# Attention mix weights spread by repeating DMAs, with the attention's branch last of four

## Chip, core and metric

The kernel runs on one core of one Trainium2 chip. The metric is the device time of one execution in microseconds. The kernel before took a median of 1982.03 us in 3 runs (1981.79 to 1984.21).

## What is computed

Two layers of a mixer over 1024 tokens and 1024 channels. In each layer a normalised input `h` is projected once; the slices feed four token mixers (Fourier, convolution, dilated attention, pooling) and a SiLU gate path for each mixer. All is float32. The part that the change touches is how three attention groups are joined:

```python
def dilated_mixture(qkv, cos, sin):
    ...
    for g, (window, dil) in enumerate(DILATED_CFG):      # three groups
        o, l = dilated_window_attention(q[:, :, g], k[:, :, g], v[:, :, g], dil, window // (2 * dil))
        outs.append(o); lses.append(l)
    alpha = jax.nn.softmax(jnp.stack(lses, axis=0), axis=0)
    out = outs[0] * alpha[0][..., None]
    for g in range(1, N_ATT_GROUPS):
        out = out + outs[g] * alpha[g][..., None]

def hybrid_layer(...):
    ...
    for n, y in enumerate(branch_outs):                  # Fourier, convolution, attention, pooling
        y_n = (y * gate_paths[:, :, n]) @ w_branch[n]
        mg = jax.nn.sigmoid(h @ w_gate[n] + b_gate[n])
        merged = mg * y_n if merged is None else merged + mg * y_n
    return x + merged @ w_out
```

`alpha` is one number per group, token and head, and each is multiplied with 64 channels of that head.

## The kernel before

Activations lie with channels on the 128 partitions and tokens along the free dimension, in two halves of 512 tokens. Every matmul in full precision is three float32r passes over a high and a low part; `split` (L104) makes these parts with one ScalarE copy and one VectorE subtraction, and is what `w`, `g`, `t`, `pl` and `wf` on L106 and L107 are.

The order within a layer (`layer`, L1161) is: the pooling and convolution inputs, six attention groups (two head pairs `hp` times three dilations `g`; each has a `q`, a `k` and a `v` unit), two Fourier units, six gate paths, four branch projections (`branch`, L951), the merge gates (`gates`, L1029) and the output projection. These main matmuls are emitted in a plain loop. All that does not lie on this main line is a generator in a lane: `pool`, `taps` (the convolution's 31 taps on VectorE, then `conv_mix` for each half), `att` (`att_tiles`: scores, softmax and weighted values of one group), `mix` (`att_mix`), `fou`, `g` (the gated input of a branch) and `forms` (sums and differences of `h` for the gates). `passes` (L124) calls `tick` after every second pair of operands, which are 6 matmuls, and a tick advances each lane by one `yield`. `finish` steps a lane to its end on the spot. The planner that puts the emitted instructions into the queues of the engines takes the order of emission as priority; loads under `high_priority` go ahead of it.

One head pair's statistics are `st` [128 tokens, 8 tiles, maximum and sum for two heads]. The dilated groups have their tokens in another order, so `st` goes through a DRAM tile `sc` and back as `nat` in token order (L564 to L574). `att_mix` (L577) then works out the three weights `e` with tokens on the partitions. To multiply them with the outputs, whose partitions are channels, it copies each weight 64 times along the free dimension (`fx`, L609), and TensorE transposes these copies in blocks of 128 by 128, four for a half and group (`fb`, L615). VectorE multiplies the group's output `og`, read back from DRAM (`od`), with that PSUM tile (L616) and adds the groups up (L618). The result is parked in DRAM (`att`).

For the branches, `gated` (L927) loads a parked mixer output (`unpark`), multiplies it with its gate path where that has not been done (`gt`, for the attention alone) and splits it (`g`). `YORDER` sets the order of the branches, here pooling (3), Fourier (0), attention (2), convolution (1). Before branch `i` the lanes that make the input of the next one are finished and its `gated` is started, so it is emitted beside branch `i`. With the third branch (`FORMS = 2`) `token_forms` (L963) starts. `branch` evacuates each PSUM tile with ScalarE to `y` (L959) and stores it from SP (L960). PSUM has 3 banks `mm` and 5 `aux`; the SBUF tiles of 512 tokens are 12 slots of one tag, `t`.

Of the kernel before, what the change touches and what calls it, by code (L numbers as in the profile page):

```python
# [9 lines left out]
F32 = mybir.dt.float32  # L10
F32R = mybir.dt.float32r
AF = mybir.ActivationFunctionType
ALU = mybir.AluOpType

P = 128
S = 1024
# [12 lines left out]
TAP = 3  # L29
LEAD = 6  # L30
ORDER = (0, 2, 1, 3)
YORDER = (3, 0, 2, 1)
FORMS = 2
NW = 4
KEPT = (None, None, None, "H", "H", "H", "H", "M")
# [12 lines left out]
class Net:  # L48
# [404 lines left out]
                self.split(hi[:, cs], lo[:, cs], ps[:, :len(part) * P])  # L453
                yield

    def att_group(self, l, hp, g, done):
        cos, sin = self.slot("cos", tag="M"), self.slot("sin", tag="M")
        for i, t in enumerate((cos, sin)):
            self.nc.sync.dma_start(out=t, in_=self.a["rope"][g, i])
        q = self.rope_unit(l, U_Q + 2 * g + hp, g, cos, sin, True)  # L460
        k = self.rope_unit(l, U_K + 2 * g + hp, g, cos, sin, False)
        vt = self.v_unit(l, U_V + 2 * g + hp, g)
        self.start("att", self.att_tiles(l, hp, g, q, k, vt, done))

    def att_tiles(self, l, hp, g, q, k, vt, done):
        nc = self.nc
        v = {}
        yield from self.wait(2)
# [78 lines left out]
        ps, pts = {}, {}  # L547
        for t in range(8 + LAG):
            if t < 8 and t % 2 == 0:
                s = products(t)  # L550
                for i in range(2):
                    ps[t + i] = scores(t + i, s[i])
            yield
            if t >= LAG:
                weighted(t - LAG, *pts.pop(t - LAG))
            if LAGT <= t < 8 + LAGT:
                pts[t - LAGT] = transposed(t - LAGT, ps.pop(t - LAGT))
            yield
        od = self.dr.tile([P, S], F32, name=f"od_{l}_{hp}_{g}")
        nc.sync.dma_start(out=od, in_=o)  # L560
        if g == 0:
            done.append((od, st))
            return
        sc = self.dr.tile([S, 4], F32, name=f"sc_{l}_{hp}_{g}")  # L564
        if g == 1:
            dst = sc.rearrange("(j p r) c -> p r j c", p=P, r=4)
            for r in range(4):
# [4 lines left out]
                nc.sync.dma_start(out=dst[two], in_=st[64 * two:64 * two + 64])  # L572
        nat = self.sm.tile([P, 8, 4], F32, tag="nat", name=f"nat{g}", bufs=4)
        nc.sync.dma_start(out=nat, in_=sc.rearrange("(t p) c -> p t c", p=P))  # L574
        done.append((od, nat))

    def att_mix(self, groups, park):  # L577

        nc = self.nc
        while len(groups) < 3:  # L580
            yield
        yield from self.wait(4)
        sm = lambda nm: self.sm.tile([P, 8, 2], F32, tag="x" + nm, name="x" + nm, bufs=2)
        ms = [st[:, :, 0:2] for _, st in groups]
        ds = [st[:, :, 2:4] for _, st in groups]
        m = sm("m")
        nc.vector.tensor_tensor(out=m, in0=ms[0], in1=ms[1], op=ALU.max)
        nc.vector.tensor_tensor(out=m, in0=m, in1=ms[2], op=ALU.max)
        es = []
        for g in range(3):  # L590
            e = sm(f"e{g}")
            nc.vector.tensor_tensor(out=e, in0=ms[g], in1=m, op=ALU.subtract)
            nc.scalar.activation(out=e, in_=e, func=AF.Exp)
            es.append(e)
        z, t = sm("z"), sm("t")
        nc.vector.tensor_tensor(out=z, in0=ds[0], in1=es[0], op=ALU.mult)
        for g in (1, 2):
            nc.vector.tensor_tensor(out=t, in0=ds[g], in1=es[g], op=ALU.mult)
            nc.vector.tensor_tensor(out=z, in0=z, in1=t, op=ALU.add)
        nc.vector.reciprocal(out=z, in_=z)  # L600
        for g in range(3):
            nc.vector.tensor_tensor(out=es[g], in0=es[g], in1=z, op=ALU.mult)
        yield from self.wait(2)
        for hf in range(2):
            sl = slice(hf * H, hf * H + H)
            out = None
            for g in range(3):
                f = self.t2("fx").rearrange("p (t h c) -> p t h c", t=4, h=2)
                nc.vector.tensor_copy(out=f, in_=es[g][:, 4 * hf:4 * hf + 4].unsqueeze(3).to_broadcast([P, 4, 2, 64]))  # L609
                og = self.t2("og")  # L610
                nc.sync.dma_start(out=og, in_=groups[g][0][:, sl])
                yield from self.wait(4)
                ps = self.aux("fb")
                for j in range(4):
                    nc.tensor.transpose(ps[:, j * P:(j + 1) * P], f[:, j].rearrange("p h c -> p (h c)"), self.ident)  # L615
                nc.vector.tensor_tensor(out=og, in0=og, in1=ps, op=ALU.mult)  # L616
                if g:
                    nc.vector.tensor_tensor(out=out, in0=out, in1=og, op=ALU.add)  # L618
                else:
                    out = og  # L620
            nc.sync.dma_start(out=park[:, sl], in_=out)
# [539 lines left out]
    def layer(self, l):  # L1161
        nc = self.nc
        pool = self.pool(l)
        att = self.dr.tile([2, P, S], F32, name=f"att{l}")
        for hp in range(2):
            done = []
            for g in range(3):
                self.att_group(l, hp, g, done)
            self.start("mix", self.att_mix(done, att[hp]))
        uf = [self.fourier_in(l, c) for c in range(2)]  # L1170
        res, fy = [], []
        self.start("fou", self.fourier_pq(l, uf, res))
        self.start("fou", self.fourier_out(l, res, fy))
        conv = self.dr.tile([2, P, S], F32, name=f"conv{l}")
        gps = {0: [], 1: [], 2: []}
        four = self.dr.tile([2, P, S], F32, name=f"four{l}")
        self.start("fou", self.gate_later(fy, gps[0], four))
        for hf in range(2):
            self.start("taps", self.conv_mix(l, hf, gps[1], conv))
        tf = {i: [] for i in range(1, 5)}  # L1180
        g = {n: [] for n in range(4)}
        make = {0: self.gated(self.unpark(four), None, g[0]), 1: self.gated(self.unpark(conv), None, g[1]),
                2: self.gated(self.unpark(att), gps[2], g[2]), 3: self.gated(self.unpark(pool), None, g[3])}
        lanes = {0: ("fou",), 2: ("att", "mix"), 1: ("taps",), 3: ()}
        for n in GORDER:
            for c in range(2):
                if (n, c) == (GORDER[2], 1):
                    self.start("g", make[YORDER[0]])
                gps[n].append(self.gate_path(l, n, c))
        for i, n in enumerate(YORDER):  # L1190
            self.finish("g")
            if i < 3:
                for lane in lanes[YORDER[i + 1]]:
                    self.finish(lane)
                self.start("g", make[YORDER[i + 1]])
            if i == FORMS:
                self.start("forms", self.token_forms(tf))
            self.branch(l, n, g[n])
        self.finish("forms")
        self.out_proj(l, self.gates(l, tf))  # L1200
# [97 lines left out]
```

## Time and profile before

| | before |
|---|---|
| median of 3 runs | 1982.03 us |
| the profiled execution | 1983.95 us |
| its span, first to last instruction | 1982.2 us |
| TensorE busy | 1950.8 us (98%) |
| VectorE busy | 1485.8 us (75%) |
| ScalarE busy | 1001.1 us (51%) |
| mean granted TensorE clock | 0.998 of full speed |

The page of the profile gives the busy time of each engine, the costliest groups of instructions and the DMA issues. Matmuls overlap: what one costs TensorE is the distance to the start of the next, and not its busy time. A wait is the idle time of an engine just before an instruction, put down to what released it.

### The profile page before, as it was taken

What the parts mean: (1) busy time and instruction counts of PE and PEld (TensorE: products, weight loads), DVE (VectorE), ACT (ScalarE), POOL (GpSimd) and SP (SyncE); (2) the same over time, 40 slices, a digit from 0 to 9 for tenths busy, and PEclk for the clock granted to TensorE, in tenths of its full rate; (3) what the DMA queues carried; (4) which work ended last, traced back from release to release, by engine and by line L of the source; (5) the groups of instructions that cost most, each with busy time, mean ns of one, the idle gap of its engine ahead of it and who ended that gap; (6) DMA issues with size and microseconds to landing.
All of it is one profiled execution on the core that took longest, in us unless ns stands there. A gap on an engine that the chain in (4) does not pass through costs nothing.

```text
span 1982.2 us, 26843 instructions
## 1 busy us (share of the span) xinstructions
PE 1950.8 (98%) x9518; PEld 1629.6 (82%) x9518; DVE 1485.8 (75%) x2731; ACT 1001.1 (51%) x1911; POOL 41.2 (2%) x90
## 2 busy tenths in 40 slices
PE   9999999999999999999999999999999999999998
PEld 7788888788888888887888888888888888888788
DVE  8598888886587878776655888888564877787764
ACT  7335655567474434344421456656775644443441
POOL 0000000000000000000000000000000000000000
PEclk9999999999999999999999999999999999999999
DMA  7244343423874433427421534434248823434443
GB/s 239 78 150 125 104 131 110 129 73 102 265 277 164 143 107 113 155 79 259 161 79 50 156 119 133 131 106 114 75 148 293 282 88 125 138 98 147 169 150 107
DMA packets 129877, 281.07 MB, mean 142 GB/s; under 512 B 33360, under 2 KB 38352, under 8 KB 129744
## 3 DMA queue, kind: packets, MB, share of 16 engines
q1 hardware_dynamic: 116784, 237.29, 37.2%
q0 software_dynamic: 10944, 39.85, 6.0%
q10 hardware_dynamic: 2016, 2.23, 0.3%
q8 instruction: 75, 1.23, 0.3%
q14 instruction: 58, 0.48, 0.1%
HBM read 186.84 MB, written 67.30 MB: 128 GB/s over the span
## 4 chain that ended last, share of the span: by engine, by line
PE 82%; DVE 9%; ACT 4%; DMA 3%; issue 2%; SPq 0%; DVEq 0%; ACTq 0%
PE z L130 25%; PE ga L130 13%; PE g L130 9%; PE op L130 9%; PE gb L130 8%; PE py L130 8%; PE z L257 3%; DVE cv L870 2%; PE pv L130 2%; PE s L494 2%; PE pt L520 1%; DVE w L107 1%; ACT w L106 1%; DMA mt<-m 1%; ACT o L544 1%
## 5 line engine op out<-in xcount | busy, mean ns | idle before, releaser
L130 PE MATMUL z<-h,w 128*128 128x512 f32 x3000 | 739.6, 396 | 1.9 <-DVE gp L631 1.4
L130 PEld LDWEIGHTS z<-h,w 128*128 128x128 f32 x3000 | 547.9, 188 | 107.4 <-DVE gp L631 1.8
L107 DVE TENSOR_TENSOR w<-wr,w 128x1024 fp32r<-128x1024 f32 (+3 forms) x136 | 158.8, 1171 | 100.1 <-ACT w L106 90.9
L106 ACT ACTIVATE w<-wr 128x1024 fp32r<-128x1024 f32 (+3 forms) x136 | 137.9, 1016 | 170.4 <-PE z L130 79.3
L130 PE MATMUL gb<-t,wf 128*128 128x512 f32 x768 | 184.5, 389 | 0.0
L130 PE MATMUL g<-h,wf 128*128 128x512 f32 x768 | 184.5, 389 | 0.0
L130 PE MATMUL ga<-t,wf 128*128 128x512 f32 x768 | 184.5, 389 | 0.0
L130 PE MATMUL op<-m,w 128*128 128x512 f32 (+1 forms) x960 | 179.7, 348 | 2.4 <-DVE m L107 2.4
L870 DVE SCALAR_TENSOR_TENSOR cv<-cv,params 128x512 f32<-128x512 f32 x240 | 179.0, 746 | 2.2
L130 PE MATMUL py<-g,w 128*128 128x512 f32 x768 | 178.9, 392 | 1.1 <-DVE gp L631 0.5
L130 PEld LDWEIGHTS op<-m,w 128*128 128x128 f32 x960 | 154.0, 190 | 26.5 <-DVE m L107 3.7
L130 PEld LDWEIGHTS py<-g,w 128*128 128x128 f32 x768 | 143.2, 188 | 32.5 <-ACT y L959 2.2
L130 PEld LDWEIGHTS g<-h,wf 128*128 128x128 f32 x768 | 144.2, 188 | 29.9
L130 PEld LDWEIGHTS gb<-t,wf 128*128 128x128 f32 x768 | 144.2, 188 | 29.8
L130 PEld LDWEIGHTS ga<-t,wf 128*128 128x128 f32 x768 | 144.2, 188 | 29.8
L106 ACT ACTIVATE wf<-wr 128x512 fp32r<-128x512 f32 x144 | 90.9, 632 | 117.8 <-issue 46.5
L107 DVE TENSOR_TENSOR wf<-wr,wf 128x512 fp32r<-128x512 f32 x144 | 98.8, 686 | 19.6 <-ACT wf L106 18.4
L508 ACT ACTIVATE p<-p,nm 128x256 f32<-128x256 f32 (+1 forms) x192 | 88.8, 464 | 48.8 <-DVE nm L505 48.6
L106 ACT ACTIVATE wf<-s 128x512 fp32r<-128x512 f32 x64 | 40.4, 632 | 105.5 <-PE gb L130 62.9
L544 ACT ACTIVATE o<-pv 64x128 f32<-64x128 f32 x192 | 67.6, 352 | 50.3 <-PE pv L130 48.4
L130 PE MATMUL ga<-h,wf 128*128 128x512 f32 x384 | 92.3, 389 | 0.0
L130 PEld LDWEIGHTS ga<-h,wf 128*128 128x128 f32 x384 | 72.1, 188 | 14.9
(251 smaller groups left out, 2697.5 us busy)
## 6 DMA issues: line engine op xcount, KB each, us to landing
wr<-in_w_in_dram SPq DMA_DIRECT2D x74, 512.0 KB, 3.7
y<-y SPq DMA_DIRECT2D x128, 256.0 KB, 4.0
y<-y POOLq DMA_DIRECT2D x64, 512.0 KB, 4.8
wr<-in_w_gate_dram SPq DMA_DIRECT2D x48, 512.0 KB, 4.3
wr<-in_w_out_dram SPq DMA_DIRECT2D x32, 512.0 KB, 3.5
rot<-rt SPq DMA_DIRECT2D x192, 64.0 KB, 2.0
cv<-in_w_gate_dram SPq DMA_DIRECT2D x16, 512.0 KB, 5.1
wr<-in_w_branch_dram SPq DMA_DIRECT2D x16, 512.0 KB, 5.0
```

Source lines behind the costliest of these rows:

```text
L106: self.nc.scalar.activation(out=hi, in_=src, func=AF.Copy)
L107: self.nc.vector.tensor_tensor(out=lo, in0=src, in1=hi.bitcast(F32), op=ALU.subtract)
L130: self.nc.tensor.matmul(ps, w, x, start=(first and i + u == 0), stop=(i == n - 1 and u == 2), skip_group_check=open_)
L257: self.nc.tensor.matmul(ps, a[:, k], b, start=(k + j == 0), stop=(k == KC - 1 and j == 2))
L494: mm(s[i][h], q[h + j][:, qs], k[h][:, a:a + n], start=(j == 0), stop=(j == 2))
L508: nc.scalar.activation(out=ph, in_=ph, func=AF.Exp, bias=nm[:, h:h + 1], accum_out=st[:, t, 2 + h:3 + h])
L520: nc.tensor.transpose(pt[:, cs], p[:, off:off + P], self.ident)
L544: nc.scalar.activation(out=dst, in_=src, func=AF.Copy)
L870: self.tc.keep_in_program_order(nc.vector.scalar_tensor_tensor(out=y, in0=u[:, j:j + H], scalar=tap(j), in1=y, op0=ALU.mult, op1=ALU.add))
```

## The change

The softmax weights of a head pair (now one tile `ea` for three groups) are transposed once, [128 tokens, 48] to [48, 128 tokens], copied to SBUF (`er`) and stored in a DRAM tile `ed`, one row of 128 tokens for each group, tile and head. For each half and group two DMAs read the four rows of a head 64 times, so that `f` comes with channels on the partitions, and VectorE multiplies it with `og`. The `fx` copies and `fb` transposes are gone, and the three `Exp` are one. The token-order round trip of `st` becomes `by_token`, called after the last scores of a group (`t == 6`) instead of behind its last tile, so that `att_mix` waits for the statistics (`sts`) first and for the outputs (`done`) later. Its waits, in ticks, change. `YORDER` puts the convolution's branch third and the attention's last.

```diff
-YORDER = (3, 0, 2, 1)
+YORDER = (3, 0, 1, 2)
...
@@ att_tiles
                     ps[t + i] = scores(t + i, s[i])
+                if t == 6:
+                    self.by_token(st, f"{l}_{hp}_{g}", g, sts)
             yield
...
         nc.sync.dma_start(out=od, in_=o)
+        done.append(od)
+
+    def by_token(self, st, name, g, sts):
+        nc = self.nc
         if g == 0:
-            done.append((od, st))
+            sts.append(st)
             return
...
-        done.append((od, nat))
-
-    def att_mix(self, groups, park):
-        nc = self.nc
-        while len(groups) < 3:
+        sts.append(nat)
+
+    def att_mix(self, sts, groups, park, name):
+        nc = self.nc
+        while len(sts) < 3:
             yield
-        yield from self.wait(4)
+        yield from self.wait(10)
...
-        es = []
+        ea = self.sm.tile([P, 3, 8, 2], F32, tag="xe", name="xe", bufs=2)
+        es = [ea[:, g] for g in range(3)]
         for g in range(3):
-            e = sm(f"e{g}")
-            nc.vector.tensor_tensor(out=e, in0=ms[g], in1=m, op=ALU.subtract)
-            nc.scalar.activation(out=e, in_=e, func=AF.Exp)
-            es.append(e)
+            nc.vector.tensor_tensor(out=es[g], in0=ms[g], in1=m, op=ALU.subtract)
+        nc.scalar.activation(out=ea, in_=ea, func=AF.Exp)
...
-        yield from self.wait(2)
+        yield from self.wait(6)
+
+        ps = self.aux("et")
+        nc.tensor.transpose(ps[:48, 0:P], ea.rearrange("p g t h -> p (g t h)"), self.ident)
+        er = self.t2("er")
+        nc.scalar.activation(out=er[:48, 0:P], in_=ps[:48, 0:P], func=AF.Copy)
+        ed = self.dr.tile([3, 8, 2, P], F32, name=f"ed_{name}")
+        nc.sync.dma_start(out=ed.rearrange("g t h p -> (g t h) p"), in_=er[:48, 0:P])
+        while len(groups) < 3:
+            yield
         for hf in range(2):
             sl = slice(hf * H, hf * H + H)
             out = None
             for g in range(3):
-                f = self.t2("fx").rearrange("p (t h c) -> p t h c", t=4, h=2)
-                nc.vector.tensor_copy(out=f, in_=es[g][:, 4 * hf:4 * hf + 4].unsqueeze(3).to_broadcast([P, 4, 2, 64]))
-                og = self.t2("og")
-                nc.sync.dma_start(out=og, in_=groups[g][0][:, sl])
-                yield from self.wait(4)
-                ps = self.aux("fb")
-                for j in range(4):
-                    nc.tensor.transpose(ps[:, j * P:(j + 1) * P], f[:, j].rearrange("p h c -> p (h c)"), self.ident)
-                nc.vector.tensor_tensor(out=og, in0=og, in1=ps, op=ALU.mult)
+                f, og = self.t2("fx"), self.t2("og")
+                for h in range(2):
+                    nc.sync.dma_start(out=f[64 * h:64 * h + 64].rearrange("p (t n) -> p t n", n=P),
+                                      in_=ed[g, 4 * hf:4 * hf + 4, h].unsqueeze(0).to_broadcast([64, 4, P]))
+                nc.sync.dma_start(out=og, in_=groups[g][:, sl])
+                yield from self.wait(3 if hf or g else 6)
+                nc.vector.tensor_tensor(out=og, in0=og, in1=f, op=ALU.mult)
```

## Rows read from the trace of the kernel before

**Rows 1.** The page, busy time (share) and instructions of each engine.

```profile
PE 1950.8 (98%) x9518; PEld 1629.6 (82%) x9518; DVE 1485.8 (75%) x2731; ACT 1001.1 (51%) x1911; POOL 41.2 (2%) x90
```

**Rows 2.** Table by stretches: busy us (instructions) per engine, clock, DMA share, GB/s.

```profile
300.00:400.00 100.00, 97.45 (x534) 81.82 (x533) 83.15 (x195) 53.42 (x134) 0.00 (x0) 1.00 0.39 115
...
520.00:540.00 20.00, 20.00 (x96) 16.51 (x95) 7.69 (x11) 9.54 (x16) 0.00 (x0) 1.00 0.95 308
...
600.00:900.00 300.00, 300.00 (x1326) 248.54 (x1324) 232.56 (x357) 123.78 (x191) 17.48 (x33) 1.00 0.38 128
...
1540.00:1560.00 20.00, 20.00 (x90) 16.58 (x89) 20.00 (x34) 13.01 (x24) 1.06 (x2) 1.00 0.72 232
```

**Rows 3.** Waits of PE: who waited for whom, us in total, times, longest.

```profile
PE pv L130 <- DVE pl L107: 2.2, 3, 0.8
...
PE fb L615 <- DVE fx L609: 1.4, 2, 1.0
...
PE fb L615 <- ACT o L544: 0.8, 2, 0.4
...
PE py L130 <- ACT y L959: 0.4, 2, 0.2
```

**Rows 4.** Chain that ended last in order of time: start, us, what.

```profile
1523.78 48.58 PE py L130 x213
```

**Rows 5.** The tile `fb`: count, ns min/median/max, starts; then what waits ended on.

```profile
L615 PE MATMUL fb<-consts,fx x96: 269/273/332, 317.7 to 1506.2; 128*128 128x128 f32 x96
L616 DVE TENSOR_TENSOR og<-og,fb x24: 674/682/689, 319.5 to 1506.5; 128x512 f32<-128x512 f32 x24
...
  DMA og<-od: 5.9, 3
```

**Rows 6.** Timeline of PE, 1500 to 1530: start, us, instruction.

```profile
1505.90 0.60 PE L615 MATMUL fb<-consts,fx 128*128 128x128 f32 x4
1506.25 17.30 PE L130 MATMUL py<-g,w 128*128 128x512 f32 x75
```

**Rows 7.** The tile `xe`: its widening copy to `fx`.

```profile
L609 DVE COPY fx<-xe x24: 411/420/428, 313.3 to 1498.1; 128x512 f32<-128x512 f32 x24
```

**Rows 8.** DMA: queues, issues with median us to landing, then L611 (issue ns).

```profile
q1 hardware_dynamic: 116784, 237.29, 37.2%
...
q10 hardware_dynamic: 2016, 2.23, 0.3%
...
att<-og SPq DMA_DIRECT2D x8, 256.0 KB, 2.5
...
unpark<-att SPq DMA_DIRECT2D x8, 256.0 KB, 6.1
...
sc<-st SPq DMA_DIRECT2D x16, 4.0 KB, 1.6
...
L611 SPq DMA_DIRECT2D og<-od x24: 326/426/1108, 310.6 to 1501.2; - x24
...
DMA to landing us min/median/max: 2.6/3.8/6.9
```

**Rows 9.** Waits of SP's queue: us in total, times, longest.

```profile
SPq L117 <- DVE w L107: 301.8, 85, 23.6
...
SPq L568 <- DVE st L503: 42.5, 10, 13.0
```

**Rows 10.** Timeline of PE, 500 to 512: end of `conv_mix`, first branch.

```profile
503.31 0.40 PE L130 MATMUL cp<-csh,w 128*128 128x512 f32 x1
...
508.12 1.52 PE L130 MATMUL py<-g,w 128*128 128x512 f32 x6
```

**Rows 11.** DVE: the multiply `gt`, its wait (us, times, longest), first weight form.

```profile
L938 DVE TENSOR_TENSOR gt<-unpark,gp x8: 684/686/694, 538.8 to 1520.9; 128x512 f32<-128x512 f32 x8
...
DVE gt L938 <- DMA unpark<-att: 10.3, 3, 5.4
...
601.01 0.69 DVE L107 TENSOR_TENSOR wf<-s,wf 128x512 fp32r<-128x512 f32 x1 [5.05 <-ACT wf L106]
```

More of the change, by code (lines that the diff above doesn't have):

```diff
@@ L454, in v_tiles, with att_group @@
                 yield
-    def att_group(self, l, hp, g, done):
+    def att_group(self, l, hp, g, done, sts):
         cos, sin = self.slot("cos", tag="M"), self.slot("sin", tag="M")
@@ L462, in att_group, with att_tiles @@
         vt = self.v_unit(l, U_V + 2 * g + hp, g)
-        self.start("att", self.att_tiles(l, hp, g, q, k, vt, done))
-    def att_tiles(self, l, hp, g, q, k, vt, done):
+        self.start("att", self.att_tiles(l, hp, g, q, k, vt, done, sts))
+    def att_tiles(self, l, hp, g, q, k, vt, done, sts):
         nc = self.nc
@@ L560, in att_tiles @@
         nc.sync.dma_start(out=od, in_=o)
+        done.append(od)
+    def by_token(self, st, name, g, sts):
+        nc = self.nc
         if g == 0:
-            done.append((od, st))
+            sts.append(st)
             return
-        sc = self.dr.tile([S, 4], F32, name=f"sc_{l}_{hp}_{g}")
+        sc = self.dr.tile([S, 4], F32, name=f"sc_{name}")
         if g == 1:
@@ L574, in att_tiles @@
         nc.sync.dma_start(out=nat, in_=sc.rearrange("(t p) c -> p t c", p=P))
-        done.append((od, nat))
-    def att_mix(self, groups, park):
+        sts.append(nat)
+    def att_mix(self, sts, groups, park, name):
         nc = self.nc
-        while len(groups) < 3:
+        while len(sts) < 3:
             yield
-        yield from self.wait(4)
+        yield from self.wait(10)
         sm = lambda nm: self.sm.tile([P, 8, 2], F32, tag="x" + nm, name="x" + nm, bufs=2)
-        ms = [st[:, :, 0:2] for _, st in groups]
-        ds = [st[:, :, 2:4] for _, st in groups]
+        ms = [st[:, :, 0:2] for st in sts]
+        ds = [st[:, :, 2:4] for st in sts]
         m = sm("m")
@@ L1165, in layer @@
         for hp in range(2):
-            done = []
+            done, sts = [], []
             for g in range(3):
-                self.att_group(l, hp, g, done)
-            self.start("mix", self.att_mix(done, att[hp]))
+                self.att_group(l, hp, g, done, sts)
+            self.start("mix", self.att_mix(sts, done, att[hp], f"{l}_{hp}"))
         uf = [self.fourier_in(l, c) for c in range(2)]
```

## The prediction

> **What bounds the kernel now.** I read the page first: TensorE (PE) is busy for 1950.8 of 1982.2 us, VectorE (DVE) for 75% and ScalarE (ACT) for half [rows 1]. The table by stretches then shows where that holds [rows 2]: in the gates (600 to 900) PE is busy for all 300 us; in the attention (300 to 400) for 97.45 of 100 with DVE at 83; in the branch projections for 20.00 of 20 us both at 520 to 540, where the DMA engines are 0.95 busy, and at 1540 to 1560 in the second layer, where DVE too has 20.00 of 20. The granted clock is 1.00 in all of them, the 2.4 GHz level. PE's own waits are small: the largest that touch this change are 1.4 us for `fx`, 0.8 us for the evacuation that frees a bank for `fb`, and 0.4 us in `py` for `y` [rows 3]. So a PE instruction taken out is worth the time until the next one starts, and one more wait of PE costs its whole length.
>
> **How time is counted in the code.** All lanes advance by one yield per tick, and a tick comes once per 6 main matmuls. 213 `py` in 48.58 us [rows 4] give 0.228 us for one and 1.37 us for a tick. A half unit has 4 ticks, a branch 16. I count ticks from the start of the first attention unit in the first layer: six groups of 24 (144), two Fourier units (160), six gate paths (208), then four branches ending at 224, 240, 256 and 272.
>
> **Removed: the transposes.** 24 groups of four `fb` (96 in all) [rows 5]. One `fb` shows 273 ns busy, but they overlap. A group that starts at 1505.90 is followed by the next `py` at 1506.25 [rows 6]: four in 0.35 us, and the 24 pairs of this kind look alike. As the times are rounded I take 0.355: 24 x 0.355 = 8.5 us of PE. Where the page and the row differ: the Trainium skill ("TensorE: Matmul & The Clock Gate", Part 4: PE-mode transpose) puts a transpose in a kernel at some 275 ns; the busy time here agrees, the starts do not, at 89 ns each. By its figure the sum would start from an estimated 26 us.
>
> **Removed beside it.** 24 `fx` copies of 0.42 us leave DVE (10.1 us) [rows 7], and 8 of 12 small `Exp` leave ACT. DVE's multiply by `fb` stays, reading `f` from SBUF; `gt`, a multiply of two SBUF tiles of the same size, takes 0.686 us against its 0.682 [rows 5, 11], so no difference. The two waits of `fb`, 2.2 us in all [rows 3], go with it; what is late next there is `pv` or `pt`, whose inputs come from the same DVE and ACT. I count 1.0 us of it as gained, with bounds of 0 and 2.2. The lighter DVE might relieve PE's `pv` waits for `pl` (2.2 us [rows 3]); I count nothing, and up to 1.5 us in the range.
>
> **Added on PE and ACT.** Four transposes of 48 rows. No such operation is in the trace; the nearest is one `fb` (89 ns from start to start), and a lone one with nothing behind it could cost its 273 ns [rows 5]. Between 0 and 1.1 us; I take 4 x 0.09 = 0.4 us, since matmuls follow it directly. The four `er` copies on ACT stand against the eight `Exp`; 0.
>
> **Added on the queues.** Per mix 12 DMAs for `f` and one for `ed`, on SP: 52 in all. Issuing one `og` took a median of 0.43 us [rows 8], so 22 us of SP over the run, some 6 us per mix in about 29 us (21 ticks). Each `f` DMA writes 64 x 4 packets of 512 B: 12288 packets. Bounds: the SP queue's mean packet of 2.03 KB cost 0.372 x 16 x 1982.2 / 116784 = 101 ns; a quarter of it is 25 ns; the nearest row is ACT's queue, 1.1 KB in some 47 ns [rows 8]. So 25 to 47 ns, or 4.8 to 9.0 us of all 16 engines per mix. The trace shows no DMA that reads a row 64 times; I take the cheap end, since the bytes halve again from the nearest row. Hidden by: the attention's DMA share, 0.39 in 300 to 400 [rows 2]. If the cover is gone (0.95 in 520 to 540 [rows 2]) `y` stores land later; that is in the range.
>
> **Added waits.** SP holds the first `f` until `ed` has landed (`sc`, the smallest store, lands in 1.6 us, `att` in 2.5 [rows 8]): at most some 2.5 us per mix, with rope halves and weight loads queued behind it. SP already stands for 301.8 us over 85 weight loads, since their buffers are full [rows 9], so this is cover; cost 0. The multiply waits in DVE's queue for `f`: with 3 ticks (4.1 us), for the first of a mix 6 ticks (8.2 us) between issue and use. Two 128 KB DMAs and `og`: `og`, as large as both, lands in 3.8 us [rows 8], but `f` has one issue of 0.43 ahead of its second half. That fits narrowly. Behind the multiply stand `pl`, `st` and `rot` on DVE, and PE's `pv` and `s` wait for those.
>
> **Moved: the `sc` DMAs** go from the end of `att_tiles` to its step 6. SP waits for `st` there already (42.5 us over 10 [rows 9]), so the compiled order had them early; cost 0. The mix counts from the third `st` (tick 182) instead of the third `od` (194): 182 + 10 + 6 = 198, then 6 + 5 x 3 = 219 for its last multiply, where it was 194 + 4 + 2 + 24 = 224. The trace agrees: the last `cp` start at 503.31 and the branches at 508.12 [rows 10], tick 204 and 208.
>
> **Moved: the attention branch last.** The convolution must now be parked by tick 224 instead of 240. Its lane has 4 x 42 + 2 x 18 = 204 yields, so 20 ticks are left; cost 0. The attention's result is wanted at 240 instead of 224: five ticks become 21, where before there were none. That cures DVE's 10.3 us behind `unpark<-att` and the ACT `y` copies held behind it; but PE lost only 0.4 us to `y` [rows 3, 11], so the gain is 0.4. The price: four `gt` multiplies per layer (0.69 us each, 2.7 us) now run beside the token forms, where DVE is full [rows 2]. ACT's `y` copies stand in one queue with splits that wait for these forms, and PE waits for banks. After the forms DVE idles for 5.05 us before the first weight form [rows 11]: the 2.7 us fit before the gates. What may surface is the bank wait in the branches: 0 to 2.7 us per layer. I take 1.0 each, 2.0 us.
>
> **The sum.** -8.5 + 0.4 - 1.0 - 0.4 + 2.0 = -7.5 us. The profiled execution took 1983.95 us (span 1982.2 and 1.75 around it), 0.1% over the median of 1982.03. 1983.95 - 7.5 = 1976.4 there, 1974.5 us against the median.
>
> **Rivals.** *The freed time comes back as idle.* Half of the groups (12, 4.3 us) run inside the attention, where DVE is 83% busy and PE waits for `pl`. If DVE sets the pace there, -7.5 becomes -3.2: 1978.8. For it: nearly all of PE's idle is in that stage [rows 2]. Against it: DVE itself gives up 10.1 us. *Forms push back.* If all of the 2.7 us reach PE in both layers, 5.4 replaces 2.0: 1977.9. For it: DVE at 20.00 of 20 us; against it: the 5 us of slack behind. *Late weights block DVE (the slower case).* If `f` lands as late as `unpark<-att` did (6.1 us [rows 8]), five multiplies per mix hold DVE for 2.0 us each: 10 us, of which some 3.5 are idle there anyway, 6.5 x 4 = 26 us: 2000.5. It decides from a landing of about 5.4 us: five holds of 1.3 us less 3.5 are 3 us a mix, 12 in all. For it: DVE waited for `og<-od` three times (5.9 us [rows 5]). Against it: `og` lands in 3.8. *Transposes cost what they are busy.* If each `fb` held PE for its 273 ns, 26.2 us replace 8.5: 1956.8; the next matmul would then start 1.1 us after a group's first and not 0.36. By the skill's section named above it would come out so; the trace speaks against it.
>
> **How the numbers follow.** Forecast 0.63, idle 0.17, forms 0.10, late weights 0.08, busy transposes 0.02. I take 0.2%, 4 us, as what a measurement of this kernel can tell from no change. Forecast, busy transposes and half of the forms' case are faster (0.70), idle and the other half the same (0.22), late weights slower (0.08). Low end: -8.5 - 2.2 - 0.4 - 1.5 = -12.6, 1969.5. High end: beyond the idle case, with the high bound of four transposes and some 2 us for crowded DMA: 1982.0. Outside lie the slower case, the busy transposes and some of the forecast's tails.
>
> **What would show it.** Right: no `fb`, PE busy some 8 us shorter, its idle time near the 31 us of before, `f` landing under 4 us, few holds of `og` on DVE. Wrong: holds of `og` for `f` of more than some 14 us a mix; PE waits for `pl`, `st` or `rot` grown by 4 us or more; `py` waiting for `y` in the last two branches; SP standing long before an `f` while a weight load is queued behind it.

## The result and the profile after

The changed kernel took a median of 2002.49 us (2000.48 to 2007.26, 4 runs), the kernel before 1982.20 us on the same chip: a ratio of 1.0105, 95% interval [1.0093, 1.0118]. It is about 20 us slower, where 7.5 us less was forecast and 1982.0 us was the top of the range. The profiled execution took 2001.32 us, its span is 1999.5 us, and 0.996 of the full clock was granted on average, against 0.998.

The page after, busy time (share) and instructions of each engine; it answers to [rows 1]:

```profile
PE 1947.1 (97%) x9426; PEld 1621.9 (81%) x9426; DVE 1476.6 (74%) x2707; ACT 994.7 (50%) x1904; POOL 41.1 (2%) x90
```

The 92 instructions are gone, but TensorE's busy time fell by 3.7 us only, and its idle time rose from 31.4 us (1982.2 less 1950.8) to 52.4: -3.7 + 21.0 is the 17.3 us by which the span grew. TensorE's waits after (who waited for whom, us in total, times, longest) say where; in [rows 3] the first of these stood at 0.4:

```profile
PE py L130 <- ACT y L972: 18.0, 14, 3.0
PE z L130 <- ACT vt L433: 4.2, 4, 1.5
PE pv L130 <- DVE pl L107: 2.8, 5, 0.8
...
PE py L130 <- ACT g L106: 1.4, 1, 1.4
...
PE py L130 <- DVE g L107: 1.3, 3, 0.8
```

The branches' matmuls `py` wait for ScalarE's copies of `y`, which free the PSUM banks. Dating the stages confirms it. The first `py` and the first gate matmul of each layer in the timelines of TensorE, before (the start in layer 0 is in [rows 10]):

```profile
599.66 2.88 PE L130 MATMUL g<-h,wf 128*128 128x512 f32 x12
...
1482.16 1.53 PE L130 MATMUL py<-g,w 128*128 128x512 f32 x6
...
1572.19 2.88 PE L130 MATMUL g<-h,wf 128*128 128x512 f32 x12
```

and after:

```profile
506.04 0.49 PE L130 MATMUL py<-g,w 128*128 128x512 f32 x1 [1.44 <-ACT g L106]
...
611.20 2.88 PE L130 MATMUL g<-h,wf 128*128 128x512 f32 x12
...
1492.57 1.84 PE L130 MATMUL py<-g,w 128*128 128x512 f32 x7
...
1590.78 2.88 PE L130 MATMUL g<-h,wf 128*128 128x512 f32 x12
```

Up to the branches of layer 0 the span gains 2.1 us, with 2.2 of the new 4.2 us of `vt` inside. Those branches go from 91.5 to 105.2 us: 13.6 lost. From there to the branches of layer 1 another 1.1 us is gained (881.37 us for 882.50, with the other 1.9 us of `vt` inside). The branches of layer 1 go from 90.0 to 98.2 us: 8.2 lost. The rest gains 1.3. So, set against the kernel before, the loss lies in two stretches of some 100 us, which held the second mix of each layer; all that lies outside them (span less branches) goes from 1800.6 to 1796.1 us, a gain of 4.5.

The table by stretches, columns as in [rows 2]:

```profile
520.00:540.00 20.00, 14.85 (x64) 11.62 (x64) 9.14 (x13) 12.40 (x22) 0.00 (x0) 1.00 0.82 279
...
565.00:570.00 5.00, 5.00 (x24) 4.14 (x23) 4.58 (x6) 2.01 (x3) 0.00 (x0) 1.00 0.56 150
...
575.00:580.00 5.00, 4.31 (x16) 2.84 (x14) 3.44 (x7) 1.97 (x4) 0.00 (x0) 0.77 0.77 279
...
1555.00:1560.00 5.00, 2.31 (x6) 1.83 (x7) 4.96 (x9) 3.31 (x7) 0.00 (x0) 0.69 0.74 285
1560.00:1565.00 5.00, 5.00 (x16) 3.95 (x15) 4.97 (x10) 3.42 (x8) 0.00 (x0) 0.63 0.27 105
```

Where TensorE was kept 20.00 of 20 us at 520 to 540, it now has 14.85, and the DMA engines are less busy there than before (0.82 for 0.95): they are not what is short. A second loss rides on the first in two places. From 575 and from 1560, behind waits of TensorE, the mean granted clock of 5 us is 0.77 and 0.63, and 16 matmuls pass in 5 us where 24 do at full clock. The mean clock of the run fell by 0.002, which is an estimated 4 us of the span; that would explain why the busy time fell by 3.7 us and not by 8.

How `y` comes late is read first from the earliest such stretch, in layer 0, on four queues. VectorE's multiplies wait for the mix's operands (start, us, instruction, [idle before <- releaser]):

```profile
516.64 0.69 DVE L629 TENSOR_TENSOR og<-og,fx 128x512 f32<-128x512 f32 x1 [5.67 <-DMA og<-od]
...
520.37 0.69 DVE L629 TENSOR_TENSOR og<-og,fx 128x512 f32<-128x512 f32 x1 [1.84 <-DMA og<-od]
521.10 0.69 DVE L631 TENSOR_TENSOR og<-og 128x512 f32<-128x512 f32 x1
```

SP's queue, in its order:

```profile
516.53 0.45 SPq L973 DMA_DIRECT2D y<-y  x1
521.82 0.32 SPq L634 DMA_DIRECT2D att<-og  x1
522.18 1.26 SPq L625 DMA_DIRECT2D fx<-ed  x2
523.48 0.60 SPq L627 DMA_DIRECT2D og<-od  x1
524.43 0.32 SPq L960 DMA_DIRECT2D unpark<-four  x1
```

ScalarE's queue:

```profile
520.87 0.63 ACT L106 ACTIVATE g<-unpark 128x512 fp32r<-128x512 f32 x1 [10.04 <-DMA unpark<-four]
...
522.88 1.55 ACT L972 ACTIVATE y<-py 128x512 f32<-128x512 f32 x3
528.21 0.63 ACT L106 ACTIVATE g<-unpark 128x512 fp32r<-128x512 f32 x1 [3.78 <-DMA unpark<-four]
...
530.01 3.51 ACT L972 ACTIVATE y<-py 128x512 f32<-128x512 f32 x7
```

and TensorE:

```profile
523.50 4.39 PE L130 MATMUL py<-g,w 128*128 128x512 f32 x18 [2.40 <-ACT y L972]
530.64 4.62 PE L130 MATMUL py<-g,w 128*128 128x512 f32 x19 [2.75 <-ACT y L972]
```

The sum `out` of the mix ends at 521.8. SP stands until then (4.8 us) to issue the store `att<-og`. The loads of the Fourier output for the next branch, ready in DRAM long ago, stand behind that store, two `fx` and an `og`; `unpark<-four` is issued at 524.43. ScalarE reaches the split of that load and waits until 528.21, with the `y` copies of finished PSUM banks behind it in its own queue. TensorE waits for a bank until 530.64. The first of the four loads had been late too, at 515.11 behind two rounds of `fx` and `og`. Before, the loads were ahead of this store. In the branches of both layers SP stood for such stores 2.8 us before and 11.9 after. Its queue before in the same stretch, the last of the four loads and the store:

```profile
515.90 0.37 SPq L947 DMA_DIRECT2D unpark<-four  x1
...
518.78 0.32 SPq L621 DMA_DIRECT2D att<-og  x1
```

This stretch and what follows it cost 6.3 of the 18.0 us of waits for `y` (2.40 and 2.75 us above, and 1.17 at 549.12), all in layer 0. The other 11.7 us lie in the last 45 us of the branches, 6.3 in layer 0 and 5.4 in layer 1, where the longest is

```profile
1557.69 19.72 PE L130 MATMUL py<-g,w 128*128 128x512 f32 x72 [2.99 <-ACT y L972]
```

There the mixed output is long ready: its last stores are issued at 539.55 and 1518.84, the first loads of it at 559.83 and 1539.29. What ScalarE stands for are the split of `gt`, for which VectorE waits for `unpark<-att`, and the split of the branch weights `wr`. In SP's queue these loads stand behind the stores of `y` and behind each other; here in layer 0, two weight loads that keep SP for 6.12 us, with parked loads behind them:

```profile
549.10 10.16 SPq L973 DMA_DIRECT2D y<-y  x13
...
559.83 0.41 SPq L960 DMA_DIRECT2D unpark<-att  x1
560.29 6.12 SPq L117 DMA_DIRECT2D wr<-in_w_branch_dram  x2
566.46 0.42 SPq L960 DMA_DIRECT2D unpark<-att  x1
```

The waits of the same kinds over the run, after; in [rows 5] the first was 5.9, in [rows 11] the second 10.3:

```profile
DVE og L629 <- DMA og<-od: 33.0, 10, 5.9
...
DVE gt L951 <- DMA unpark<-att: 27.7, 6, 11.4
...
SPq L634 <- DVE og L631: 22.4, 8, 4.8
...
ACT g L106 <- DMA unpark<-four: 16.8, 6, 10.0
...
ACT g L106 <- DMA unpark<-conv: 13.3, 5, 5.5
```

and the tile `fx` after:

```profile
L625 SPq DMA_DIRECT2D fx<-ed x48: 573/616/1385, 314.2 to 1512.3; - x48
...
DMA to landing us min/median/max: 2.8/4.1/7.7
```

All ten holds of `og` lie in the branch stages, none in the attention. The landing does not make the difference: `fx` landed in 2.8 to 7.7 us in the attention and in 3.0 to 5.4 in the branches. Its issue does. In the stretch above two `fx` and an `og` are issued only behind the store at 521.82, and VectorE stands for them until 526.93.

### The profile page after: what moved, and what is told of

The parts are those of the page before. It is cut to its first block, busy times and chain, and to the rows that moved or that the text cites. A ratio compares the mean times of both kernels' runs of the same rounds, so it can differ in the third digit from the quotient of the medians.

```text
span 1999.5 us, 26669 instructions
## 1 busy us (share of the span) xinstructions
PE 1947.1 (97%) x9426; PEld 1621.9 (81%) x9426; DVE 1476.6 (74%) x2707; ACT 994.7 (50%) x1904; POOL 41.1 (2%) x90
## 4 chain that ended last, share of the span: by engine, by line
PE 77%; DVE 10%; DMA 5%; ACT 4%; issue 2%; SPq 1%; DVEq 0%; ACTq 0%
PE z L130 24%; PE ga L130 13%; PE g L130 9%; PE op L130 8%; PE gb L130 8%; PE py L130 4%; PE z L257 3%; DVE cv L883 3%; PE pv L130 2%; PE s L494 1%; PE pt L520 1%; DVE w L107 1%; DMA unpark<-att 1%; ACT w L106 1%; PE pq L130 1%
## 5 line engine op out<-in xcount | busy, mean ns | idle before, releaser
L130 PE MATMUL py<-g,w 128*128 128x512 f32 x768 | 184.4, 399 | 20.7 <-ACT y L972 18.0
L107 DVE TENSOR_TENSOR wf<-wr,wf 128x512 fp32r<-128x512 f32 x144 | 98.8, 686 | 19.4 <-ACT wf L106 18.3
L106 ACT ACTIVATE wf<-s 128x512 fp32r<-128x512 f32 x64 | 40.5, 632 | 105.2 <-PE gb L130 62.6
```

Of the source, the lines that this page charges most:

```text
L106: self.nc.scalar.activation(out=hi, in_=src, func=AF.Copy)
L107: self.nc.vector.tensor_tensor(out=lo, in0=src, in1=hi.bitcast(F32), op=ALU.subtract)
L130: self.nc.tensor.matmul(ps, w, x, start=(first and i + u == 0), stop=(i == n - 1 and u == 2), skip_group_check=open_)
```

## The experiments

Times are set against the kernel before on the same chip. "The branches" are the two stretches dated above (91.5 and 90.0 us before, 105.2 and 98.2 after). Moving a DMA to another queue, or its emission, also lets the planner order the rest of SP's queue a little differently; only where the text says so is that order the same.

### The parts of the change by themselves

The kernel before with the new order of the branches alone (e2), and the kernel after with the old one (e1):

```diff
-YORDER = (3, 0, 2, 1)
+YORDER = (3, 0, 1, 2)
```

> The kernel before with only the order of branches changed (convolution third, attention last). Queue: no f DMAs, so 1979 to 1986 us, within 0.2% of before. Order: the attention's gating beside the forms costs here as in the changed kernel, 1990 to 2002. Traffic: 1982, no change.

Measured: 1987.58 us, 1.0034 [1.0022, 1.0045]; branches 94.9 and 92.7. The order alone costs about 7 us. TensorE's wait for `y`:

```profile
PE py L130 <- ACT y L959: 5.1, 9, 0.8
```

All nine lie in the last 45 us of the branches, 3.1 us in layer 0 and 2.0 in layer 1.

> The changed kernel with the attention's branch third and the convolution's last again, as before. Three theories. Queue: the second mix's f, og and att DMAs stand in SP's queue in the branch stage, and the loads of mixer outputs and branch weights behind them come late, so ACT's splits wait and its y copies behind these keep PE's banks full. Then the order of the branches hardly matters: 1996 to 2006 us, with py still waiting for y by over 12 us. Order: the attention's gating beside the token forms is what costs. Then this run falls to 1974 to 1982. Traffic: the 512 B packets crowd the DMA engines. Then about 2002, like the queue theory; this run does not tell those two apart.

Measured: 2000.6 us, 1.0097 [1.0082, 1.0112]; branches 102.9 and 99.6. In the kernel after, taking the order back gives nothing that can be told from zero: the order is not the main loss, and its price does not add to the other.

The kernel after without the 48 DMAs that spread the weights; the weights are left out of the sum and `og` is multiplied by itself (e4):

```diff
-                f, og = self.t2("fx"), self.t2("og")
-                for h in range(2):
-                    nc.sync.dma_start(out=f[64 * h:64 * h + 64]...
+                og = self.t2("og")
...
-                nc.vector.tensor_tensor(out=og, in0=og, in1=f, op=ALU.mult)
+                nc.vector.tensor_tensor(out=og, in0=og, in1=og, op=ALU.mult)
```

> The changed kernel without the f DMAs; VectorE multiplies og with itself, so the softmax weights are left out of the sum (ed is still written). og and att stay on SP. Queue: 12 of 20 DMAs of each mix leave SP's queue, 1973 to 1984 us. Order: about 2000. Traffic: 1972 to 1978. Together with the run that issues the mix from POOL it separates queue from traffic: fast in both is the queue, fast here alone is the traffic.

Measured: 1974.93 us, 0.9971 [0.9960, 0.9983]; branches 94.0 and 90.8; waits for `y` 6.5 us. So the 48 DMAs, with the tiles they fill and the wait for `ed`, cost 1.0105 - 0.9971 = 0.0134, some 26.5 us, and that is about the whole miss. In the profiled executions 18.6 us of it lie in the branches and 7.2 outside them (1788.9 us for 1796.1). Against e2 (the same order, with the transposes) e4 is 12.5 us shorter, with some 3 us of uncertainty: this agrees with the 9.5 us expected of transposes and waits, though the two kernels differ in more than these.

### By which queue they cost it

Four runs move one group of DMAs each from SP to GpSimd's queue. First all of the mix, that is `f`, `og` and the store `att` (e3):

```diff
-                    nc.sync.dma_start(out=f[...]...
-                nc.sync.dma_start(out=og, in_=groups[g][:, sl])
-            nc.sync.dma_start(out=park[:, sl], in_=out)
+                    nc.gpsimd.dma_start(out=f[...]...
+                nc.gpsimd.dma_start(out=og, in_=groups[g][:, sl])
+            nc.gpsimd.dma_start(out=park[:, sl], in_=out)
```

> The changed kernel with the f and og loads and the att store of the mix issued from POOL's queue instead of SP's; the bytes and the packets are the same. Queue: SP's order in the branch stage is then free of the mix, and the gain of the transposes comes through: 1972 to 1982 us, py waiting for y by less than 4 us. Order: about 2000. Traffic: about 2000, since the same packets run on the same DMA engines.

Measured: 1984.69 us, 1.0024 [1.0013, 1.0035]; branches 95.6 and 96.6; waits for `y` 6.5 us, but 5.4 for the split `g` of VectorE. Some 16 of 20 us come back, although `f` now lands later (median 5.7 us): the same transfers on the same DMA engines, in another queue.

Then the branch weights alone, to see whether their late loads are the link (e5):

```diff
-            wh, wl = self.load_unit(self.a["w_branch"][l, n, u])
+            wh, wl = self.load_unit(self.a["w_branch"][l, n, u], queue=self.nc.gpsimd)
```

> The changed kernel with the mix left on SP, but the 16 loads of branch weights issued from POOL's queue. If the late weight loads (three of them behind 13 y stores in SP's queue) carry the last two branches' loss, this falls by half, to 1988 to 1994, and what is left are the loads of the Fourier and convolution outputs behind the mix's store. If the loss is the mix's traffic or the order of the branches, it stays at 1996 to 2005.

Measured: 2002.77 us, 1.0107 [1.0090, 1.0124]; `y` 18.9 us. Nothing in the sum, but the waits for `y` have moved: in the last 45 us of the branches they fall from 11.7 to 5.5 us, about what e2 has there, and ahead of these they rise from 6.3 to 13.4, where ScalarE's waits for `unpark<-four` grow to 23.9 us. So the weights, that I had named in the prediction's last sign, are a link late in the branches; alone they give nothing back, since the parked loads are still held.

The store of the mixed output alone, the instruction that SP stands for (e9):

```diff
-            nc.sync.dma_start(out=park[:, sl], in_=out)
+            nc.gpsimd.dma_start(out=park[:, sl], in_=out)
```

> The changed kernel with only att's two stores per mix issued from POOL. In the trace of the change SP stands 22.4 us before these stores, waiting for VectorE's add, which waits for og and f, and the loads of the Fourier output are queued behind. If this store is the link, the first two branches lose some 8 us less: 1988 to 1995. If the 12 f and 6 og DMAs themselves (0.62 and 0.59 us of SP each) are enough, it stays at 1997 to 2004.

Measured: 1990.82 us, 1.0047 [1.0032, 1.0062]; branches 97.9 and 94.9; `y` 8.5 us, of which 6.7 in the last 45 us of the branches. About 11 us come back, so the store holds the loads behind it late in the branches too.

And the loads behind it alone, with the whole mix left on SP (e14):

```diff
-            self.nc.sync.dma_start(out=t, in_=park[c, :, sl])
+            self.nc.gpsimd.dma_start(out=t, in_=park[c, :, sl])
```

> The changed kernel, the mix left on SP, but the loads of the parked mixer outputs issued from POOL. If PE's loss is ACT's queue standing for these loads behind the mix's store in SP's queue, this is as good as moving the store away: 1985 to 1992. If the y stores or the branch weights behind the mix are the loss, it stays at 1996 to 2004.

Measured: 1984.51 us, 1.0013 [1.0004, 1.0022]; branches 94.3 and 94.8. Some 18 us come back. Its waits:

```profile
PE py L130 <- ACT y L972: 6.6, 11, 1.5
...
SPq L634 <- DVE og L631: 20.4, 8, 4.6
...
DVE og L629 <- DMA og<-od: 26.8, 9, 8.8
...
ACT g L106 <- DMA unpark<-four: 6.0, 2, 5.6
```

and the stretch that lost most in layer 0, columns as above:

```profile
520.00:540.00 20.00, 20.00 (x89) 16.54 (x89) 7.70 (x11) 11.95 (x23) 2.15 (x4) 1.00 0.96 340
```

This is the run that decides. SP stands for the mix as long as in the kernel after (20.4 us for 22.4) and VectorE for its operands almost as long (26.8 for 33.0), but no load of a parked output is queued behind, and most of the lost time is back. TensorE is kept 20.00 of 20 us with the DMA engines 0.96 busy, so traffic was not the loss. Neither hold costs much by itself; what is behind SP's does. The kernel before with this edit was not run; TensorE's waits before its `py` were 0.9 us in all, so the edit had little to give there. Of the 6.6 us of waits for `y` that are left, 5.1 lie in the last 45 us of the branches, as in e2. Outside the branches little is gained (1793.2 us for 1796.1).

Both kinds of loads, parked outputs and weights, on GpSimd (e15):

> As the run before it in this call, and the branch weights on POOL too: what stands behind the mix in SP's queue is then only y's stores. If all of the loss goes through loads that come late behind the mix: 1978 to 1986, with no more than the order's 5 us and the packets' 4 us left over the gain. If SP's 18 DMAs per mix hold y's stores and by them the slots: 1993 to 2003.

Measured: 1989.87 us, 1.0040 [1.0025, 1.0055]; `y` 8.2 us; 5 us worse than the parked outputs alone. That the two kinds of load now wait for each other in GpSimd's queue is a guess that was not traced further.

### Why the mix is late: rows, number, pace

The weights stored with a head's tokens in one row, so that `f` reads 2 KB rows in place of four of 512 B, with the same DMAs in the same order on SP (e10):

```diff
-        ed = self.dr.tile([3, 8, 2, P], F32, name=f"ed_{name}")
+        ed = self.dr.tile([3, 2, S], F32, name=f"ed_{name}")
...
-                                      in_=ed[g, 4 * hf:4 * hf + 4, h].unsqueeze(0).to_broadcast([64, 4, P]))
+                    nc.sync.dma_start(out=f[64 * h:64 * h + 64], in_=ed[g, h, sl].unsqueeze(0).to_broadcast([64, H]))
```

> The changed kernel with the weights stored with each group's and head's tokens in one row, so that an f DMA repeats one row of 2 KB 64 times (64 packets) and not four rows of 512 B (256 packets). Same bytes and same count of DMAs, and SP's queue holds the same order of instructions. The run with plain rows fell by 17 us, but its SP order had changed too. If the packets' size is the cost: 1983 to 1991. If it was the order, or reading one row 64 times: 1996 to 2004.

Measured: 1997.85 us, 1.0086 [1.0069, 1.0103]; `y` 14.5 us. The tile `fx`, VectorE's holds and the landing:

```profile
  DMA og<-od: 30.5, 10
...
DMA to landing us min/median/max: 2.7/3.8/7.6
```

A quarter of the packets makes some 4 us, at the edge of what the intervals can tell apart. Packet size is a small part.

As many DMAs, but reading plain rows of 2 KB from `od` (e6):

```diff
-                                      in_=ed[g, 4 * hf:4 * hf + 4, h].unsqueeze(0).to_broadcast([64, 4, P]))
+                    nc.sync.dma_start(out=f[64 * h:64 * h + 64], in_=groups[g][64 * h:64 * h + 64, sl])
```

> The changed kernel with each f DMA replaced by one of the same size and count that reads plain rows of 2 KB from od (64 packets in place of 256, no row read twice); the weights are left out, og is multiplied with itself. Queue, by the number of DMAs: 1995 to 2004, hardly better than the change. Queue or traffic by the packets (an f DMA takes 0.62 us to issue, and each brings 256 packets of 512 B): 1980 to 1990.

Measured: 1985.73 us, 1.0022 [1.0013, 1.0031]; `y` 10.7 us. This can't be put down to the repeated row: `f` no longer carries the weights or depends on `ed`, and the planner put SP's queue into another order in many places. It stays open.

Six ticks between load and use everywhere (e8):

```diff
-                yield from self.wait(3 if hf or g else 6)
+                yield from self.wait(6)
```

> The changed kernel with 6 ticks ahead of every multiply of the mix, not 3; by the count of ticks its last multiply is then at 198 + 36 = 234, still ahead of 240. If the lead was too short (VectorE held by f, then att's store, then SP), the early part of the loss goes: 1988 to 1995. If it is the place of these DMAs in SP's queue, whatever their lead, it stays at 1997 to 2004.

Measured: 1991.21 us, 1.0050 [1.0035, 1.0065]; branches 100.1 and 97.0; `y` 10.3 us. 11 us come back, in the profile about half of it outside the branches (1790.5 us for 1796.1). This points to three ticks being too few; the later emission also reorders the queue.

### Parts joined

These seven join edits shown above and a pace of 4 ticks: old order, long rows, and one group of DMAs on GpSimd. "Outside" is the span of the profiled execution less the branches.

| run | edits | us | ratio, interval | branches | outside | wait for `y` |
|---|---|---|---|---|---|---|
| e7 | mix on GpSimd, old order | 1984.67 | 1.0017 [1.0007, 1.0027] | 93.6, 95.6 | 1793.6 | 4.1 |
| e11 | long rows, old order, pace 4 | 1992.34 | 1.0053 [1.0038, 1.0068] | 101.9, 96.8 | 1787.4 | 14.5 |
| e12 | e7 with long rows | 1983.37 | 1.0012 [1.0002, 1.0021] | 94.4, 97.4 | 1790.2 | 5.3 |
| e13 | e12 with pace 4 | 1983.95 | 1.0014 [1.0004, 1.0024] | 96.1, 97.0 | 1791.1 | 6.3 |
| e16 | store on GpSimd, long rows, old order | 1993.80 | 1.0062 [1.0047, 1.0077] | 101.4, 96.8 | 1795.3 | 12.3 |
| e17 | parked loads on GpSimd, long rows, old order | 1984.73 | 1.0026 [1.0015, 1.0037] | 95.2, 91.6 | 1796.1 | 6.7 |
| e18 | e17 with pace 4 | 1981.69 | 1.0005 [0.9996, 1.0015] | 100.3, 91.9 | 1787.6 | 11.4 |

> The changed kernel with the mix's DMAs on POOL and the order of the branches of before. The new order cost 7 us in the kernel before, and with the mix on POOL the change stood 4 us over it. If queue and order are two separate costs, 1974 to 1980 us. If the order costs only where SP is crowded, no better than 1984.

> Long rows, the old order of branches and 4 ticks ahead of each multiply (last one at 198 + 6 + 20 = 224, as before the change), all on SP. If a longer lead takes SP's stand before the att store away: 1976 to 1986. If 18 loads of a mix on SP in the branch stage cost by their place alone: 1990 to 2000.

> Long rows, the old order of branches, the mix's loads and stores on POOL. Against the run with the mix on POOL and the old order (1984.7) only the packets differ. If packets cost on any queue: 1974 to 1980, better than before. If they cost on SP's queue alone: 1982 to 1987.

> Long rows, old order of branches, the mix on POOL, and 4 ticks ahead of each multiply in place of 3. With 3 ticks VectorE stood up to 10.5 us before one multiply of the second layer, and PE waited 3.4 us there for a split of the gate input behind it. If that hold is what keeps the transposes' gain back: 1973 to 1979, faster than before. If the traffic of the mix in the branch stage keeps it back on any queue: 1981 to 1986.

> The changed kernel with three parts undone at once that each showed a cost: att's store on POOL (it gave 12 us), rows of 2 KB (4 us), the old order of branches (5 us in the kernel before, 2 in the changed one). If they are separate costs: 1978 to 1984. If they overlap: 1985 to 1991.

> Three edits together: the loads of the parked outputs issued by GpSimd, the mix weights stored a head to a row and read 2 KB at a time, and the old order of the branches. If what each gave alone adds up (18 us for the loads, 4.5 us for the rows, 2 us for the order), the time is 1975 to 1979 us, below the kernel before. If the loads alone already took away the holds that the other two shorten, nothing more comes and it stays at 1983 to 1986 us. TensorE's wait for the copies of y is under 5 us in the first case, 6 us or more in the second.

> The same three edits with four ticks in place of three between the load of the mix weights and their use. If the weights' landing is still what VectorE stands for, its wait for them goes and the time falls below the run with three ticks by 2 us or more. If the slower pace only pushes the last mixes into the conv and the gates, it is the same or up to 3 us longer.

What gave 18, 4 and up to 7 us alone does not add up: e17 is no better than e14, and e16 no better than e9. The best, e18, equals the kernel before and no run that keeps the mix's true weights beats it. e17 and e18 show part of the reason: they differ in the pace alone, and the fourth tick takes 8.5 us from what lies outside the branches, where TensorE's 4.2 us of waits for `vt` are gone, but adds 5.4 us to the branches. With the mix on GpSimd (e12 and e13) the fourth tick gives nothing outside. The branches of e17 with the rest of e18 would make a span of 1974.4 us, an estimate from two executions; no run had both. In e18 one wait of 7.28 us stands out in layer 0, and it is the same link with another transfer behind it. VectorE's, SP's and ScalarE's rows, then TensorE's (VectorE's wait is put down to a store of `y` there):

```profile
532.52 0.69 DVE L629 TENSOR_TENSOR og<-og,fx 128x512 f32<-128x512 f32 x1 [5.99 <-DMA y<-y]
...
533.96 0.32 SPq L634 DMA_DIRECT2D att<-og  x1
...
534.81 1.15 SPq L117 DMA_DIRECT2D wr<-in_w_branch_dram  x2
...
542.46 1.06 ACT L106 ACTIVATE w<-wr 128x1024 fp32r<-128x1024 f32 x1 [5.26 <-DMA wr<-in_w_branch_dram]
...
546.00 38.81 PE L130 MATMUL py<-g,w 128*128 128x512 f32 x160 [7.28 <-ACT y L972]
```

With the parked loads out of the way, the weights of the next branch stand behind the store, are issued at 534.81, and ScalarE waits for them with the `y` copies behind it.

## Why the prediction was wrong, step by step

**What bounds the kernel.** Right, and the reason for the size of the loss: TensorE has no slack, so the new waits of `py` came through in full (20.7 us after, the three rows above, for 0.9 before), and the clock took an estimated 4 us more.

**The transposes, -8.5, and the `fb` waits, -1.0.** Right as far as the runs can tell, though no run takes out the transposes alone: e4 against e2 gives 12.5 us with 3 of uncertainty. Busy transposes as a rival (-26.2) are ruled out by that. In the kernel after only 4.5 us were gained outside the branches, where e4 gains 11.7.

**The queues, 0: the step that failed.** The sum has two sentences here. "This is cover; cost 0" leaned on the 301.8 us that SP stands over weight loads [rows 9]. Of those only 10.7 lie in the branches, where SP has 8 weight loads a layer, and there such a stand is a hold itself, 6.12 us for two of them with parked loads behind. SP also carries the stores of `y`, the parked loads and the second mix there. And I asked what a held `f` delays (weight loads, rope halves), but not what the six rounds of `f` and `og` and the store behind them push back. SP's wait for that store hardly grew over the run (19.1 to 22.4 us), but 18.3 of the 19.1 had been in the attention of layer 1; in the branches it grew from 2.8 to 11.9, and the parked loads, which had been ahead of it, fell behind it. Removing the 48 DMAs gives back 26.5 us (e4), moving only the parked loads 18 (e14). Of what was on SP, issuing one `f` took 0.62 us and not 0.43, so 48 of them are 30 us in place of 21.

**The landing of `f`, "that fits narrowly".** The size of the landing was right: a median of 4.1 us, as long as the three ticks, and up to 7.7. What was wrong is that I took three ticks from the emission as three ticks from the issue. In the branches the loads are issued late, and all ten holds of VectorE lie there, though none of these `f` took more than 5.4 us to land. A pace of six ticks gives back 11 us (e8). The packet size, where I took the cheap end, is worth some 4 us (e10).

**The moved branch, -0.4 + 2.0.** The sign was right, the size was not: about 7 us in e2. The bank waits behind the forms are there as drawn up, 3.1 and 2.0 us in e2 and 2.5 in each layer of e14, near the 2.7 of the "forms push back" rival, taken at 1.0. The rest of e2's 7 us was not traced further. That 21 ticks would cure VectorE's 10.3 us behind `unpark<-att` was right by itself: 3.1 us are left in e2. In the kernel after it is 27.7, since these loads are issued behind the row of `y` stores and the weight loads in SP's queue; with the weights on GpSimd (e5) it is 4.7, with the store there (e9) 3.5.

**The slower rival, 2000.5.** The time is near, but that is luck: the mechanism was only half of it. VectorE did hold for `f` (33.0 us), but not by landings above its point of 5.4 us, and the price was to be paid by VectorE's queue, in all four mixes, through `pl`, `st` and `rot`. In the two mixes of the attention no multiply was held, and in e14 VectorE holds 26.8 us at 18 us less time. What paid in the branches was SP's queue: store, weight loads, parked loads, ScalarE's split, `y`, bank. It was given 0.08, because I priced each hold on the engine where it occurs and not on the queue behind the next instruction that waits for it.

**The idle rival.** It came in part. TensorE's waits in the attention did grow, by 4.2 us for `vt` that were not there before, about the size of that rival's idle, though only 1.1 us more than before were spent on VectorE's `pl`. They show in the 2.1 and 1.1 us gained on the way to the two branch stages, where the seven groups removed in each would have given 2.5. With a pace of four ticks (e18) these waits are gone, and what lies outside the branches is 8.5 us shorter than in e17; without the 48 DMAs (e4) it is 7.2 us shorter than in the kernel after. So the mixes in the attention were not free either. Why `vt` is copied late there was not traced.

**What was to show it wrong.** Two of the four signs appeared as written: holds of `og`, 16.5 us in each mix of the branches, and `py` waiting for `y` in the last two branches. SP stood not before an `f` (9.3 us over the run, 2.0 the longest) but before the store behind it. The waits for `pl` and `st` grew by 3.0 us, not by 4.

**The range.** Its ends, added up again, are 1969.4 and 1981.5 in place of 1969.5 and 1982.0; 2002.49 lies outside either way.

**What stays open.** Why the parts do not add up beyond what e17 and e18 show, since nearly every edit reorders SP's queue; why `vt` comes late at three ticks; how much of e6 is the plain row; and whether a kernel without any of these holds would keep the 8.5 us, which no run with true weights reached.

## What to carry to other kernels

Before a transfer that waits for compute is put, or made later, on a queue, list what stands behind it there in that very stage, and follow each of them to the next in-order queue: here late stores and weight loads held loads that were ready, these held a ScalarE split, and that held the copies that free PSUM banks. Cover is local: a queue's slack over a whole run says nothing of the 100 us where the new waits fall. Costs of queue order do not add up, so the combination has to be run as well as its parts.

## What the runs showed of the hardware

A transfer's issuing queue mattered more than the transfer: the same loads in GpSimd's queue in place of SP's gave back 18 us (e14). The Trainium skill ("DMA: Bandwidth & Descriptors", "Issuing engines are not separate DMA queues" and the rules at its end) holds that spreading DMAs over the issuing engines does not help bandwidth and only saves issue time. No run here tests that for bandwidth. For time the runs go further: e9 moves eight stores that take 0.32 us each to issue, 2.6 us in all, and 11 us come back, because SP no longer stands for the mix with other loads behind it.

A DMA that repeats a row 64 times took 0.62 us to issue from SP, and 0.56 with rows of 2 KB (e10). A plain `og` took 0.59 beside it, where the same load had taken 0.43 in [rows 8], so most of the 0.62 is not the repeating. Why `og` takes longer to issue now was not traced.

The granted clock was 1.00, the 2.4 GHz level, until TensorE stood idle for 2.99 us ahead of 1557.69; from 1557 to 1563 it was 0.50, the 1.2 GHz level, and from 1564 again 1.00. The same came behind the waits at 572, with 0.50 from 574 to 577. The waits of 2.40 and 2.75 us at 523.50 and 530.64 were not followed by a fall: the clock stayed at 1.00 from 520 to 540. So some of the waits in the branches were paid for a second time, not each.
